# Remainders of split weights: subtracted on GpSimd in place of VectorE

## The chip, the cores and the metric

The kernel runs on one core of a Trainium2 chip. A core has a tensor engine (PE, with its weight loads shown apart as PEld), a vector engine (DVE, VectorE), a scalar engine (ACT, ScalarE), a GpSimd engine (POOL) and a sync engine (SP) that here issues the transfers. Each engine works through its own list of instructions in order; waits between engines are semaphores. The metric is the device time of one launch in microseconds (us), median of several runs. Three runs of the kernel before took 1236.23 us at the median (1233.64 to 1236.44).

## The reference

Four residual blocks on an input of 512 tokens by 1024 features, all in float32: attention (8 forgetting heads and 8 stick-breaking heads of width 64), a gated MLP of inner width 2816 with a causal depthwise convolution of three taps, a gated short convolution, and a second such MLP.

```python
h = x
for layer in range(2):
    h = h + (attention_mixer if layer == 0 else short_conv_mixer)(h, ...)
    h = h + conv_ffn(h, ffn_norm[layer], ffn_w_up[layer], ffn_conv[layer], ffn_w_down[layer])
# conv_ffn: u = causal_dwconv(rms_norm(h) @ w_up);  g, val = halves of u;  (silu(g) * val) @ w_down
# attention_mixer: one input projection, q and k normed per head, softmax with decay (FoX) or
#   stick-breaking weights, o @ w_out.  short_conv_mixer: (B * conv3(C * u)) @ w_out
```

Every product is `activation @ weight`, with weights that come from device memory once.

## The kernel before, in words

Activations stay on chip with features on partitions and the 512 tokens along the free axis. A float32 product runs on the tensor engine as three single-pass products of halves. A number x is split into hi, its rounding to a shorter float (float32r), and lo = x - hi, the remainder. Then x @ w is hi_x hi_w + lo_x hi_w + hi_x lo_w, summed in PSUM. `mm3` (lines 237 to 239) and `mm3_rhs` (lines 480 to 482) issue these three; the one that reads the weights' remainder is line 239 or line 481.

The weights come in 198 chunks of 128 partitions by 1024 numbers (16 have 896, two have 1056). `load` (lines 211 to 227) handles one chunk in three steps: SP issues the transfer into a buffer `raw` (line 220), ScalarE rounds it into `whi` (line 223), and VectorE subtracts to give `wlo` (line 226). Each of the three names has three buffers, so the rounding of a chunk waits until the tensor engine has read the last of the chunk three before. `weights` (line 229) hands out the next chunk and first calls `load` for those up to two chunks ahead (`AHEAD = 2`). A chunk is used for 24 products of 512 columns in most stages.

The stages in order of time: input and first projections (to about 50 us), attention (to about 305 us), the first MLP (to 674), the short convolution (to 854), and the second MLP (to the end, its down projection from 1101). That last down projection works on tokens by partition in two halves of 11 double rows each; the last three chunks of a half are used together, once for each of four blocks of tokens, so that chunk 10 of a half is needed two chunks' first uses after chunk 8 and not two whole chunks later.

In attention, generators of projections ("fillers") are woven between the score blocks by counted microseconds (`after`, `fill`, `spend`); which instruction stands where on an engine is set by the order in which the program emits them, and by the tile framework's own ordering. The weights of a block of 128 queries go from VectorE (line 596 for a forgetting head, lines 603 and 604 for a stick-breaking one) to the tensor engine, which transposes them (line 623); ScalarE and VectorE split the result into `pt` (lines 626 and 627), and line 642 and 643 multiply it with the values. Norms take an inverse root on VectorE (`rsqrt`, lines 300 to 318, some ten tiny instructions); the tensor engine spreads the first of them at line 278.

GpSimd has little to do: constants at the start, eight small transfers that it issues itself (lines 107 to 114), one clearing for the gates (line 434) and 64 clearings of a part of `pt` (line 617), each of which waits until the tensor engine has finished with that buffer.

Of the kernel before, what the change touches and what calls it, by code (L numbers as in the profile page):

```python
"""Two-layer hybrid decoder trunk on one core.

Activations stay on chip, features on partitions and tokens along the free axis.
Float32 products run on the tensor engine as three single-pass products of exact
halves: x = hi + lo with hi the rounding to float32r and lo the exact remainder,
x @ w = hi_x hi_w + lo_x hi_w + hi_x lo_w, summed in float32 in PSUM.
The RMS scale of a block's input is applied to the products, so that the tensor
engine doesn't wait for it.
"""
# [40 lines left out]
def trunk(  # L50
# [21 lines left out]
    def f32(ap):  # L72
        return ap.bitcast(F32)
# [25 lines left out]
    # a row a column of `gains`: the norms after the first and the conv taps  # L99
# [67 lines left out]
    def behind(later, earlier):  # L167
        """Issues `later` after `earlier`, of the same engine."""
        tc.add_manual_dep(
            later.ins, earlier.ins.name,  # L170
            mybir.DependencyInfo(mybir.DependencyClass.NoSync, mybir.DependencyReason.DATA), reason="order",
        )

    # ---- order of the tensor engine's work: `spend` counts the microseconds that were
    # emitted, `after` puts work that waits for other engines behind some of them, and
    # `fill` emits independent products in between ----
# [33 lines left out]
    def load(i, last=None):  # L210
        dram, k0, nk, parts = wanted[i]
        n = sum(parts[1::2])
        raw = wp.tile([P, CHUNK], F32, tag="raw", name=f"raw{i}")
        hi = wp.tile([P, CHUNK], F32R, tag="whi", name=f"whi{i}", bufs=3)
        lo = wp.tile([P, CHUNK], F32R, tag="wlo", name=f"wlo{i}", bufs=3)
        v = raw[:, 0:nk * n].rearrange("p (k c) -> p k c", c=n)
        to = 0
        for c0, width in zip(parts[::2], parts[1::2]):
            with nc.allow_non_contiguous_dma(reason="eight columns"):
                nc.sync.dma_start(  # L220
                    v[:, :, to:to + width], dram[k0 * P:(k0 + nk) * P, c0:c0 + width].rearrange("(k p) c -> p k c", p=P))
            to += width
        made = act.activation(hi[:, 0:nk * n], raw[:, 0:nk * n], AF.Copy)  # L223
        if last is not None:
            behind(made, last)
        dve.tensor_tensor(lo[:, 0:nk * n], raw[:, 0:nk * n], f32(hi[:, 0:nk * n]), op=ALU.subtract)  # L226
        return [t[:, 0:nk * n].rearrange("p (k c) -> p k c", c=n) for t in (hi, lo)]
# [7 lines left out]
    def mm3(acc, w, rhs, first, last):  # L235
        """acc += w.T @ rhs of two pairs of halves."""
# [10 lines left out]
    class Norm:  # L247
        """Gathers the squares of a block's input and gives its RMS scale by token:
        `col` [token, block] on partitions and `row` along the free axis on all of them."""
# [33 lines left out]
        def scaled(self, fn):  # L283
            """Runs what needs `row` when it is there."""
# [14 lines left out]
    def rsqrt(dst, v, n, name):  # L299
        """dst = v ** -0.5 by Newton's method."""  # L300
# [22 lines left out]
    def causal_conv(dst, src, tap):  # L323
        """dst[t] = tap(2) src[t] + tap(1) src[t-1] + tap(0) src[t-2]."""
# [68 lines left out]
    # ================= attention =================  # L393
# [4 lines left out]
    def choose():  # L398
        """Columns of 0 and 1 that pick the rows of `dl` and `dr`."""
# [25 lines left out]
    def log_gate():  # L425
        """The gates' log-sigmoid, its running sums on the partitions of `dl`."""
# [70 lines left out]
    def queries_keys(p):  # L497
        """Halves of the normed, gained keys and queries of heads 2p and 2p+1. A
        stick-breaking query keeps its scale apart, by token."""
# [63 lines left out]
    def logits(p, b):  # L563
        """Scores and decay of heads 2p and 2p+1 for 128 queries, and what follows up to the weights."""
# [44 lines left out]
    def turn(p, b, ws):  # L609
        """The weights, keys on partitions, in halves."""  # L610
# [19 lines left out]
    def weigh(p, half):  # L630
        """Weights by both halves of the values at once: a head's product has the one
        half on 64 partitions and the other on the rest, which are then added."""
# [98 lines left out]
    # decay: F_q - F_k of a forgetting head as a product of four rows by four. Head  # L731
    # 2p + e has them at 64 e + 4 j + p: (F_hi 1), (F_lo 1), (1 -F_hi), (1 -F_lo).
# [40 lines left out]
    # ================= gated MLP =================  # L773
# [38 lines left out]
    # ================= gated short convolution =================  # L812
# [32 lines left out]
    # ================= gated MLP, tokens on partitions at its end =================  # L845
# [59 lines left out]
```

## Time and profile before

| what | value |
|---|---|
| median of the runs (lowest to highest) | 1236.23 us (1233.64 to 1236.44) |
| profiled execution, its own time from first to last instruction (the span) | 1231.8 us |
| median of the runs above that span | 4.4 us |
| PE busy | 1214.5 us |
| DVE busy | 762.9 us |
| ACT busy | 500.7 us |
| POOL busy | 21.5 us |
| mean granted clock of the tensor engine | 0.997 |

Engines are named PE, PEld, DVE, ACT, POOL and SP. L226 is line 226 of the kernel. A group's row gives out<-in, shapes, count, busy us and mean ns of one instruction, then the idle time just before them and what ended it. A timeline's row gives start (us from the span's start), duration (us), engine, line, operation, out<-in and, in brackets, the idle time before it with what ended it. A row of the chain of work that ended last gives start, us, and what. Products are pipelined, so the busy time of one (0.39 us for 512 columns) is longer than the distance between two (0.23 us). The buffer names in rows of the profile leave out numbers.

### The profile page before, as it was taken

The page shows a single profiled execution, that of the slowest core. Times are in us where ns is not written, and L with a number is a line of the kernel's source. Part 1 is how long each engine was busy: PE and PEld are TensorE (multiplying, and loading weights), DVE is VectorE, ACT ScalarE, POOL GpSimd, SP SyncE. Part 2 cuts the span into 40 slices and gives each one's busy share as a digit, 9 for nine tenths or more (in the row PEclk, how much of TensorE's full clock was granted, in tenths as well). Part 3 has the DMA queues.
Part 4 walks back from the last instruction along what each step waited for, and adds up shares of the span by engine and source line. Part 5 has one row for each costly group of instructions (what it writes and reads, how often), then busy time and mean ns, then how long its engine had stood idle before and what let it go on. Part 6 is the DMA issues. An engine that isn't in the chain of part 4 may idle for free.

```text
span 1231.8 us, 14998 instructions
## 1 busy us (share of the span) xinstructions
PE 1214.5 (99%) x5861; PEld 987.9 (80%) x5861; DVE 762.9 (62%) x1256; ACT 500.7 (41%) x779; POOL 21.5 (2%) x104
## 2 busy tenths in 40 slices
PE   8999999999999999999999999999999999999998
PEld 7887878767888888888888888888888888888886
DVE  5786878887776777673333555555767776762222
ACT  6455665655443434342222222233444434342120
POOL 3000000000000000000000000000000000000000
PEclk9999999999999999999999999999999999999999
DMA  6312121212333332323333333332333333322330
GB/s 177 104 36 69 36 69 36 69 52 69 95 93 100 89 102 86 103 79 95 94 94 101 91 97 99 89 101 87 91 98 92 96 95 93 98 91 86 118 105 35
DMA packets 183463, 108.13 MB, mean 88 GB/s; under 512 B 4604, under 2 KB 176684, under 8 KB 183392
## 3 DMA queue, kind: packets, MB, share of 16 engines
q1 hardware_dynamic: 183136, 107.01, 29.5%
q8 instruction: 46, 0.75, 0.3%
q0 software_dynamic: 256, 0.16, 0.1%
q14 instruction: 25, 0.20, 0.0%
HBM read 105.06 MB, written 2.10 MB: 87 GB/s over the span
## 4 chain that ended last, share of the span: by engine, by line
PE 94%; DVE 4%; ACT 1%; DMA 1%; issue 0%; SPq 0%; DVEq 0%; ACTq 0%
PE psa L237 13%; PE psa L239 13%; PE psa L238 13%; PE psb L237 11%; PE psb L239 11%; PE psb L238 11%; PE psa L480 3%; PE psa L482 3%; PE psa L481 3%; PE psb L481 2%; PE psb L480 2%; PE psb L482 2%; PE psb L576 1%; DVE rest L603 1%; PE psc L623 1%; PE psa L642 1%
## 5 line engine op out<-in xcount | busy, mean ns | idle before, releaser
L223 ACT ACTIVATE whi<-raw 128x1024 fp32r<-128x1024 f32 (+1 forms) x198 | 208.3, 1053 | 365.9 <-PE psb L238 127.0
L226 DVE TENSOR_TENSOR wlo<-raw,whi 128x1024 fp32r<-128x1024 f32 (+1 forms) x198 | 240.1, 1213 | 162.3 <-ACT whi L223 161.4
L237 PE MATMUL psa<-hs_hi,whi 128*128 128x512 f32 x544 | 220.4, 405 | 0.5 <-DVE o L653 0.5
L239 PE MATMUL psa<-hs_hi,wlo 128*128 128x512 f32 x544 | 215.5, 396 | 0.0
L238 PE MATMUL psa<-hs_lo,whi 128*128 128x512 f32 x544 | 215.0, 395 | 0.0
L237 PE MATMUL psb<-hs_hi,whi 128*128 128x512 f32 x480 | 189.9, 396 | 0.0
L239 PE MATMUL psb<-hs_hi,wlo 128*128 128x512 f32 x480 | 189.8, 395 | 0.0
L238 PE MATMUL psb<-hs_lo,whi 128*128 128x512 f32 x480 | 188.8, 393 | 0.0
L328 DVE SCALAR_TENSOR_TENSOR u<-y,taps,u 128x510 f32<-128x510 f32 (+1 forms) x176 | 131.0, 747 | 3.0
L239 PEld LDWEIGHTS psa<-hs_hi,wlo 128*128 128x128 f32 x544 | 102.2, 188 | 24.0
L237 PEld LDWEIGHTS psa<-hs_hi,whi 128*128 128x128 f32 x544 | 102.7, 189 | 21.8 <-PE psb L582 0.6
L238 PEld LDWEIGHTS psa<-hs_lo,whi 128*128 128x128 f32 x544 | 102.6, 189 | 21.4
L238 PEld LDWEIGHTS psb<-hs_lo,whi 128*128 128x128 f32 x480 | 90.1, 188 | 21.4
L239 PEld LDWEIGHTS psb<-hs_hi,wlo 128*128 128x128 f32 x480 | 90.1, 188 | 21.4
L237 PEld LDWEIGHTS psb<-hs_hi,whi 128*128 128x128 f32 x480 | 90.3, 188 | 20.3
L779 DVE TENSOR_TENSOR y<-psb,nrow_n 128x512 f32<-128x512 f32 x44 | 30.4, 691 | 83.9 <-PE psb L239 83.9
L320 ACT ACTIVATE a<-u 128x512 fp32r<-128x512 f32 x44 | 27.8, 633 | 118.7 <-DVE u L784 118.7
L783 ACT ACTIVATE u<-u 128x512 f32<-128x512 f32 x44 | 27.8, 632 | 91.4 <-DVE u L328 91.4
L325 ACT ACTIVATE u<-y,taps 128x512 f32<-128x512 f32 x88 | 62.9, 717 | 0.0
L321 DVE TENSOR_TENSOR a<-u,a 128x512 fp32r<-128x512 f32 x44 | 30.4, 692 | 29.4 <-ACT a L320 29.4
L480 PE MATMUL psa<-whi,hs_hi 128*128 128x256 f32 (+1 forms) x128 | 38.6, 303 | 0.0
L482 PE MATMUL psa<-whi,hs_lo 128*128 128x256 f32 (+1 forms) x128 | 36.2, 283 | 0.0
(226 smaller groups left out, 1851.0 us busy)
## 6 DMA issues: line engine op xcount, KB each, us to landing
raw<-in_ffn_w_up SPq DMA_DIRECT2D x88, 512.0 KB, 3.8
raw<-in_ffn_w_down SPq DMA_DIRECT2D x30, 512.0 KB, 3.7
raw<-in_attn_w_in SPq DMA_DIRECT2D x24, 512.0 KB, 3.9
raw<-in_conv_w_in SPq DMA_DIRECT2D x24, 512.0 KB, 3.8
raw<-in_ffn_w_down SPq DMA_DIRECT2D x16, 448.0 KB, 3.7
raw<-in_attn_w_out SPq DMA_DIRECT2D x8, 512.0 KB, 3.4
raw<-in_conv_w_out SPq DMA_DIRECT2D x8, 512.0 KB, 3.9
x_tok<-in_x SPq DMA_DIRECT2D x4, 512.0 KB, 7.9
```

Source lines behind the costliest of these rows:

```text
L223: made = act.activation(hi[:, 0:nk * n], raw[:, 0:nk * n], AF.Copy)
L226: dve.tensor_tensor(lo[:, 0:nk * n], raw[:, 0:nk * n], f32(hi[:, 0:nk * n]), op=ALU.subtract)
L237: pe.matmul(acc, w[0], rhs[0], start=first, stop=False)
L238: pe.matmul(acc, w[0], rhs[1], start=False, stop=False)
L239: pe.matmul(acc, w[1], rhs[0], start=False, stop=last)
L321: dve.tensor_tensor(lo, src, f32(hi), op=ALU.subtract)
L325: act.activation(dst, src, AF.Copy, scale=tap(2))
L328: dve.scalar_tensor_tensor(dst[:, d:], src[:, 0:S - d], tap(j), dst[:, d:], op0=ALU.mult, op1=ALU.add)
L480: pe.matmul(acc, lhs[0], w[0], start=first, stop=False)
L481: pe.matmul(acc, lhs[0], w[1], start=False, stop=False)
L482: pe.matmul(acc, lhs[1], w[0], start=False, stop=last)
L779: dve.tensor_tensor(y, acc, norm.row, op=ALU.mult)
```

## The change

One line: the engine that subtracts `raw - whi` into `wlo`. The data, the sizes, the buffers and what is computed are the same; all 198 subtractions move. (The rest of the difference between the files takes comments away and is left out.)

```diff
         made = act.activation(hi[:, 0:nk * n], raw[:, 0:nk * n], AF.Copy)
         if last is not None:
             behind(made, last)
-        dve.tensor_tensor(lo[:, 0:nk * n], raw[:, 0:nk * n], f32(hi[:, 0:nk * n]), op=ALU.subtract)
+        pool.tensor_tensor(lo[:, 0:nk * n], raw[:, 0:nk * n], f32(hi[:, 0:nk * n]), op=ALU.subtract)
         return [t[:, 0:nk * n].rearrange("p (k c) -> p k c", c=n) for t in (hi, lo)]
```

GpSimd at the start of the program: the first six subtractions, among the constants, the small transfers into `spare` (lines 108 to 114) and the gates' clearing. The numbers behind names are buffers: `wlo_175` is the first chunk's remainder, `wlo_370` the fourth's.

```order
 L417 TENSOR_SCALAR cols<-cols 128x1
+L226 TENSOR_TENSOR wlo_175<-raw_173,whi_174 128x1024
+L226 TENSOR_TENSOR wlo_234<-raw_232,whi_233 128x1024
 L108 DMA spare<-in_ffn_norm 16x128
+L226 TENSOR_TENSOR wlo_240<-raw_238,whi_239 128x1056
 L109 DMA spare<-in_conv_norm 8x128
 L110 DMA spare<-in_conv_kernel 24x128
 L114 DMA spare<-in_ffn_conv 66x128 x4
+L226 TENSOR_TENSOR wlo_370<-raw_368,whi_369 128x1056
+L226 TENSOR_TENSOR wlo_426<-raw_424,whi_425 128x1024
+L226 TENSOR_TENSOR wlo_627<-raw_625,whi_626 128x1024
 L434 MEMSET fwide 128x512
```

The first two subtractions now stand ahead of all but one of the small transfers, and the third ahead of six of them.

GpSimd in attention, at the second pair of clearings (the one that is over at 91 us of the profile of before); `wlo_1349` and `wlo_1355` are the twelfth and thirteenth chunks' remainders.

```order
 L617 MEMSET pt_1275 128x128
 L617 MEMSET pt_1276 128x128
+L226 TENSOR_TENSOR wlo_1349<-raw_1347,whi_1348 128x1024
+L226 TENSOR_TENSOR wlo_1355<-raw_1353,whi_1354 128x1024
 L617 MEMSET pt_1434 128x128
 L617 MEMSET pt_1435 128x128
```

Two subtractions now stand between clearings that followed each other before; a clearing that waits for the tensor engine holds the subtractions written behind it.

VectorE in attention, at 71 us of the profile of before, where the eleventh chunk's remainder (`wlo_1000`) was made between the normed keys (`qn`) and their remainders (`qk_lo`):

```order
 L544 TENSOR_TENSOR qn_937<-qk_682,psc_932 128x512
-L226 TENSOR_TENSOR wlo_1000<-raw_998,whi_999 128x1024
+L544 TENSOR_TENSOR qn_948<-qk_723,psc_943 128x512
 L321 TENSOR_TENSOR qk_lo_940<-qn_937,qk_hi_939 128x512
-L544 TENSOR_TENSOR qn_948<-qk_723,psc_943 128x512
 L591 TENSOR_REDUCE top_979<-psb_966 128x1
+L321 TENSOR_TENSOR qk_lo_951<-qn_948,qk_hi_950 128x512
 L591 TENSOR_REDUCE top_987<-psb_967 128x1
```

The subtraction is gone from VectorE's list, and the second `qn` has moved up into its place. The other 197 go in the same way; at 184 us, for instance, one (the 22nd chunk's) stood in the middle of an inverse root's tiny instructions (between lines 316 and 312).

## The prediction, made before the changed kernel was run

> **What bounds the kernel now.** I read the page's busy times first, then busy time by stage, then the groups of the two weight steps, and last the few rows around the places where the tensor engine waits.
>
> ```profile
> span 1231.8 us, 14998 instructions
> core 0: us, PE busy (x) PEld busy (x) DVE busy (x) ACT busy (x) POOL busy (x), PEclk, DMA share, GB/s
> 0.00:50.00 50.00, 45.09 (x285) 39.68 (x286) 30.99 (x81) 29.90 (x47) 9.88 (x44) 0.97 0.55 152
> 50.00:266.00 216.00, 210.68 (x1404) 173.55 (x1403) 173.64 (x453) 128.34 (x292) 10.88 (x56) 1.00 0.19 55
> 266.00:310.00 44.00, 41.07 (x194) 32.83 (x194) 35.16 (x52) 24.46 (x42) 0.71 (x4) 0.96 0.22 64
> 310.00:1100.00 790.00, 790.00 (x3418) 638.99 (x3418) 489.77 (x639) 291.63 (x369) 0.00 (x0) 1.00 0.32 94
> 1100.00:1232.00 132.00, 127.67 (x565) 102.83 (x563) 33.35 (x33) 26.36 (x30) 0.00 (x0) 1.00 0.26 86
> L223 ACT ACTIVATE whi<-raw 128x1024 fp32r<-128x1024 f32 (+1 forms) x198 | 208.3, 1053 | 365.9 <-PE psb L238 127.0
> L226 DVE TENSOR_TENSOR wlo<-raw,whi 128x1024 fp32r<-128x1024 f32 (+1 forms) x198 | 240.1, 1213 | 162.3 <-ACT whi L223 161.4
> ```
>
> The tensor engine is the bound. From 310 to 1100 us, two thirds of the time, it is busy in every microsecond while DVE has 300 us to spare, so nothing that frees DVE can show there. What a faster DVE could give back lies in attention: 216.00 - 210.68 = 5.32 us of idle PE, and 44.00 - 41.07 = 2.93 us more up to 310, together 8.25, plus some 1.8 us for the granted clock of 0.96 in those 44. The change takes 240.1 us of work off DVE, 31% of what DVE does, and at best 10 us of it (8.25 + 1.8) were ever in the tensor engine's way. The row of L226 says the rest: DVE mostly stood waiting for the rounding (161.4 us). So the question is less what DVE gains than whether GpSimd is in time, and what it does to DVE while it works.
>
> **How long one subtraction takes on GpSimd.** No row of before shows one of this size there. The nearest:
>
> ```profile
> L617 POOL MEMSET pt<- 128x128 f32 x64 | 12.4, 222 | 221.3 <-PE psa L642 193.9 <-DVE inv L595 13.4 <-DVE ry_qk L316 13.0
> L434 POOL MEMSET fwide<- 128x512 f32 x1 | 0.5, 529 | 18.5 <-PE psc L542 18.5
> L409 POOL TENSOR_TENSOR both<-one 128x8 f32<-128x8 f32 x1 | 0.2, 213 | 0.0
> ```
>
> Writing alone costs (529 - 222) / 384 = 0.80 ns a column, and a two-operand instruction has 0.2 us of start-up. For 1024 columns that is 0.82 us a pass. If reads and write overlap fully, 1.02 us; if the two reads take turns, 1.84; if the write takes its turn too, 2.66. I take 2.25, midway between the last two, and keep 1.02 and 2.66 as ends. As a check from outside: the Trainium skill, "GPSIMD Engine Reference", section 3, gives 4497 ns for an addition of 2048 columns, so an estimate of some 2.25 us for half; no run here shows it yet.
>
> 198 x 2.25 = 446 us of a queue that was busy for 21.5, so its throughput is no limit. In the long stages nothing is due soon either: a chunk is rounded when the one three before is done, and two chunks of 24 products lie between. At 790 us / 3418 = 0.23 us a product that is 11 us, less 1.05 for the rounding. There the move costs nothing, hidden by the tensor engine's two chunks in hand. If VectorE were held for all of each subtraction there (142 chunks of 5.57 us in 790), it would lose 142 x (2.25 - 1.22) = 146 of its 300 us to spare: still cover.
>
> **Term 1, the last down projection.** Here the cover is gone. The rows are the rounding, the subtraction and the first product that reads it, at the first and the last of three such places (the second is at 1161.54):
>
> ```profile
> 1147.54 1.06 ACT L223 ACTIVATE whi<-raw 128x1024 fp32r<-128x1024 f32 x1 [4.54 <-PE psb L482]
> 1148.64 1.23 DVE L226 TENSOR_TENSOR wlo<-raw,whi 128x1024 fp32r<-128x1024 f32 x1 [4.37 <-ACT whi L223]
> 1150.38 0.40 PE L481 MATMUL psa<-wlo,a 128*128 128x512 f32 x1
> 1210.91 1.06 ACT L223 ACTIVATE whi<-raw 128x1024 fp32r<-128x1024 f32 x1 [4.54 <-PE psb L482]
> 1212.00 1.23 DVE L226 TENSOR_TENSOR wlo<-raw,whi 128x1024 fp32r<-128x1024 f32 x1 [4.37 <-ACT whi L223]
> 1213.74 0.40 PE L481 MATMUL psa<-wlo,a 128*128 128x512 f32 x1
> ```
>
> From the earliest start of the subtraction to the product are 1.74 us in both. At 2.25 the tensor engine waits 0.51 each time, 3 x 0.51 = +1.5 us. Ends: 0 at 1.02 us, 3 x 0.92 = +2.8 at 2.66. A quicker subtraction gains nothing here, since the product already ran on time.
>
> **Does GpSimd hold VectorE?** The rows that come nearest are clearings beside L596, VectorE's scaling of a forgetting head's weights:
>
> ```profile
> 102.22 1.20 POOL L617 MEMSET pt<- 128x128 f32 x4 [11.50 <-PE psa L642]
> 158.47 0.83 POOL L617 MEMSET pt<- 128x128 f32 x4 [11.83 <-PE psa L642]
> 102.08 0.49 DVE L596 TENSOR_SCALAR w<-w,inv 128x512 f32<-128x512 f32 x1
> 102.75 0.53 DVE L596 TENSOR_SCALAR w<-w,inv 128x512 f32<-128x512 f32 x1
> ```
>
> Four clearings take 0.83 us at 158 but 1.20 at 102, where they meet two L596 of 0.5 us: the two engines do take turns for something. Whether a subtraction that reads two tiles makes a VectorE instruction wait for all of it, no row shows. Bounds: VectorE loses nothing and is rid of 1.22 us, or it waits the whole 2.25, which is 1.03 more than it spent itself. I take the second for instructions that read two tiles on chip, because the row at 102 is a wait of nearly a whole instruction and not a slowing down, and keep both ends.
>
> The Trainium skill, "SBUF — State Buffer", section "Who interferes with whom", says that GpSimd and VectorE share a pair of ports as an exclusive lock, and that a VectorE instruction with two inputs in SBUF contends with a GpSimd one that reads SBUF; it also names the copy and scalar forms that the rows at 102 fit. By that rule the term below is +2.8 us; without any such turn-taking it would be -1.6.
>
> **Term 2, attention.** The places where the tensor engine now waits for VectorE with a subtraction just ahead in the chain of work:
>
> ```profile
> 71.27 1.22 DVE wlo L226
> 72.50 0.60 DVE qk_lo L321
> 77.61 0.61 PE L511 MATMUL psc<-head_ones,sq 128*128 128x2 f32 x4 [0.52 <-DVE pt L627]
> 183.95 1.23 DVE wlo L226
> 185.18 0.10 DVE ra_qk L312
> 191.49 0.49 PE L511 MATMUL psc<-head_ones,sq 128*128 128x2 f32 x3 [1.09 <-DVE pt L627]
> 276.31 1.06 ACT L223 ACTIVATE whi<-raw 128x1024 fp32r<-128x1024 f32 x1
> 277.90 0.41 DVE L321 TENSOR_TENSOR o_lo<-o,o_hi 128x256 fp32r<-128x256 f32 x1
> 278.84 0.68 DVE L627 TENSOR_TENSOR pt<-psc,pt 128x512 fp32r<-128x512 f32 x1
> 280.52 0.35 PE L643 MATMUL psa<-pt,v 128*128 128x256 f32 x1
> ```
>
> At the first two, VectorE's next instruction (L321 and L312) reads two tiles and follows the subtraction at once; held for 2.25 instead of spending 1.22, it hands on 1.03 us later each, and the tensor engine, which was already waiting, waits that much longer: +2.1. The third is new. Before, that chunk was subtracted late, after the block's last splits; on GpSimd it starts at 277.4, when the rounding ends, and L321 at 277.90 waits until 279.65, 1.75 us. The split behind it then ends at 279.52 + 1.75 = 281.27 instead of well ahead of L643 at 280.52: +0.75. Together +2.8. If nothing is held, the waits of 0.52 and 1.09 vanish, since 1.22 us leave their chain: -1.6. At the other places of idle PE in attention no subtraction stands right ahead, or the wait is small; I count nothing there.
>
> **Term 3, the start.** The fourth chunk's rounding meets the first inverse root:
>
> ```profile
> 24.04 1.10 ACT L223 ACTIVATE whi<-raw 128x1056 fp32r<-128x1056 f32 x1
> 25.40 0.16 DVE L316 SCALAR_TENSOR_TENSOR ncol_n<-rb_n,ry_n 128x4 f32<-128x4 f32 x1
> 26.70 0.60 PE L278 MATMUL psc<-ident,ncol_n 128*128 128x128 f32 x4
> ```
>
> The subtraction can start at 25.14 and hold L316 until 27.4; the tensor engine, due at L278 at 26.70, would get its input at about 27.6: +0.9. Without holding, 0. The last of GpSimd's small transfers fall behind three subtractions, at most 3 x 2.25 = 6.8 us:
>
> ```profile
> 19.70 2.09 POOL L114 DMA_DIRECT2D spare<-in_ffn_conv  x4
> 41.34 0.26 PE L142 MATMUL psc<-ident,spare 48*128 48x48 f32 x1
> ```
>
> Issued by 21.8 before, they are read at 41.34; those 20 us hide it, and it costs nothing.
>
> **The sum.** 1.5 + 2.8 + 0.9 = +5.2 us on the profiled span of 1231.8, so 1237.0. The median of the runs lies 4.4 us above that span; I carry this unchanged: 1236.2 + 5.2 = 1241.4.
>
> **Rivals.** *Nothing is held.* Then 1.5 - 1.6 + 0 = -0.1 us, 1236.1. For it speaks that clearings and plain two-tile instructions overlap freely in the timeline; against it the rows at 102.
>
> *VectorE's relief carries attention* (faster). 27 or so subtractions leave a stage where DVE is 80% busy (173.64 of 216). If all idle PE there and the half clock go, -10.0 + 1.5 = -8.5, 1227.7. It decides from 5.2 us of those 10 upward, for that pays term 1 and 0.3% of the time (3.7 us, about what a measurement here tells from no change). Against it: only 1.6 of the 8.25 stand at the two places above, where a subtraction leaves the chain.
>
> *GpSimd is much slower than 2.66 us,* through the short float it writes or by waiting itself for VectorE. Each microsecond above 2.25 costs one at three places each of terms 1 and 2 and one at the start, 7 in all: at 4 us, +17.5, 1253.7. Nothing in the rows asks for it.
>
> *The subtractions wait in GpSimd's queue.* The longest wait there is long:
>
> ```profile
> 73.78 0.35 POOL L617 MEMSET pt<- 128x128 f32 x2 [32.96 <-PE psa L642]
> 90.25 0.46 POOL L617 MEMSET pt<- 128x128 f32 x2 [0.48 <-PE psa L642]
> 92.73 1.06 ACT L223 ACTIVATE whi<-raw 128x1024 fp32r<-128x1024 f32 x1 [0.20 <-PE psa L482]
> ```
>
> A subtraction held for 33 us would stop the tensor engine for over 10. But the order puts `wlo_1000` ahead of the clearing at 73.78, and `wlo_1349`, behind the one that ends at 90.71, has its input only at 93.79. I give this price no chance of its own. The order also shows all 198 moved, so the change does what it says.
>
> **Chances.** VectorE held, 1238 to 1246: 0.58, of which 0.13 ends within 0.3%. Nothing held: 0.20, nearly all within 0.3% (0.17). Relief: 0.08, faster. A slow GpSimd: 0.14, slower. So faster 0.11, same 0.30, slower 0.59. The range 1233 to 1250 takes in the held case with both ends of the duration, the case of nothing held, and the nearer half of the slow one. The held case alone: 1238 to 1246.
>
> **What would show it.** L226 on POOL at 1.8 to 2.7 us; idle PE before L481 at three places near the end, half a microsecond each, put down to POOL; 310 to 1100 us unchanged at full PE; tiny VectorE instructions that last or wait 2 us beside a subtraction; idle PE from 50 to 310 at 10 to 12 us instead of 8.25. I am wrong if VectorE's two-tile instructions keep their durations beside POOL's L226, if attention gets shorter by more than 2 us, or if idle PE appears between 310 and 1100.

## The result, and the profile after

| kernel | median of the runs (lowest to highest) | profiled span |
|---|---|---|
| before | 1236.34 us (1233.64 to 1237.81) | 1231.8 us |
| after | 1275.37 us (1274.04 to 1277.40) | 1273.9 us |

The changed kernel takes 1.0322 times as long (95% interval 1.0305 to 1.0339), 39.0 us more. The forecast was 1241.4, with a range of 1233 to 1250. The direction was right, the size was not. The two profiled spans differ by 42.1 us, 3 more than the medians: by its span, the profile of before is of the quickest execution (1233.64 us), so differences between the two profiles overstate the change by about 3 us.

First the tensor engine's idle time over the same work. The windows of before and of after are cut some 8 us ahead of the first MLP's first gate, so that the same products, within three records, lie ahead of both cuts. Columns: the window and its length, busy us of PE, PEld, DVE, ACT and POOL with their instructions, then the granted clock, the DMA share and GB/s. The first fence is before, the second after.

```profile
0.00:310.00 310.00, 296.84 (x1881) 246.07 (x1882) 239.79 (x584) 182.69 (x380) 21.47 (x104) 0.99 0.25 72
310.00:1232.00 922.00, 917.67 (x3981) 741.81 (x3980) 523.12 (x672) 317.98 (x399) 0.00 (x0) 1.00 0.31 93
```

```profile
0.00:334.40 334.40, 301.79 (x1878) 248.15 (x1878) 238.96 (x549) 182.55 (x380) 106.71 (x139) 0.97 0.23 66
334.40:1274.00 939.60, 926.07 (x3983) 740.99 (x3983) 502.68 (x510) 311.61 (x399) 392.35 (x163) 1.00 0.31 92
```

The start and attention are 24.4 us longer. Idle time of the tensor engine makes 19.5 of it (334.40 - 301.79 = 32.61 after, 310.00 - 296.84 = 13.16 before), and 4.95 are products that ran slower (301.79 against 296.84 for the same work, clock 0.97 against 0.99). (Some 2.4 us of the 24.4 may be the difference between the two executions; see the table below.) The rest of the program is 17.6 us longer. VectorE did not become busier in either part: 238.96 against 239.79, and 502.68 against 523.12.

Now the groups of after, by line. Columns: busy us, mean ns of one, then the idle time before.

```profile
L226 POOL TENSOR_TENSOR wlo<-raw,whi 128x1024 fp32r<-128x1024 f32 (+1 forms) x198 | 477.0, 2410 | 694.9 <-ACT whi L223 673.1 <-PE psa L482 7.7 <-DVE ry_qk L316 7.3
L328 DVE SCALAR_TENSOR_TENSOR u<-y,taps,u 128x510 f32<-128x510 f32 (+1 forms) x176 | 250.2, 1424 | 109.2 <-ACT u L325 106.3
L259 DVE SCALAR_TENSOR_TENSOR hs_lo<-h,gains,hs_hi 128x512 fp32r<-128x512 f32 x24 | 46.8, 1949 | 19.6 <-ACT hs_hi L258 19.6
L596 DVE TENSOR_SCALAR w<-w,inv 128x128 f32<-128x128 f32 (+3 forms) x32 | 17.5, 547 | 0.8
L779 DVE TENSOR_TENSOR y<-psa,nrow_n 128x512 f32<-128x512 f32 x44 | 30.1, 684 | 2.8 <-ACT nrow_n L279 2.8
L627 DVE TENSOR_TENSOR pt<-psc,pt 128x128 fp32r<-128x128 f32 (+3 forms) x64 | 29.8, 484 | 11.4 <-ACT pt L626 11.1
L316 DVE SCALAR_TENSOR_TENSOR ncol_n<-rb_n,ry_n 128x4 f32<-128x4 f32 x4 | 3.1, 772 | 0.1
```

The same groups of before, where they differ or a comparison rests on them:

```profile
L328 DVE SCALAR_TENSOR_TENSOR u<-y,taps,u 128x510 f32<-128x510 f32 (+1 forms) x176 | 131.0, 747 | 3.0
L316 DVE SCALAR_TENSOR_TENSOR ncol_n<-rb_n,ry_n 128x4 f32<-128x4 f32 x4 | 0.6, 162 | 0.1
L259 DVE SCALAR_TENSOR_TENSOR hs_lo<-h,gains,hs_hi 128x512 fp32r<-128x512 f32 x24 | 17.9, 746 | 2.4 <-ACT hs_hi L258 2.4
L596 DVE TENSOR_SCALAR w<-w,inv 128x128 f32<-128x128 f32 (+3 forms) x32 | 12.1, 386 | 0.5
L627 DVE TENSOR_TENSOR pt<-psc,pt 128x128 fp32r<-128x128 f32 (+3 forms) x64 | 30.2, 485 | 7.8 <-ACT pt L626 7.3
```

A subtraction takes 2.41 us on GpSimd. VectorE's instructions with two inputs in tiles on chip last longer where they meet one, by up to that much: L328, the convolution's taps, takes 1424 ns on average (747 before), L259 takes 1949 (746), and of four tiny L316 on four columns one took 2.61 us, so that their mean is 772 ns (162 before). L596, which has one tile and one number for each partition, is longer too (547 ns, 386 before). L779 and L627, whose first input (`psa`, `psc`) lies in PSUM, kept their durations (L779 had 690 before), although six of the L627 began while a subtraction ran. L784 and the L321 of the gated product have two inputs on chip and kept their 0.69 us; none of these began while a subtraction ran.

Two places show what such a hold costs. VectorE and GpSimd of after, an inverse root at 196 us:

```profile
196.31 2.26 DVE L314 TENSOR_TENSOR rb_qk<-ra_qk,rh_qk 128x16 f32<-128x16 f32 x1
198.60 0.17 DVE L316 SCALAR_TENSOR_TENSOR ry_qk<-rb_qk,ry_qk 128x16 f32<-128x16 f32 x1
196.10 2.44 POOL L226 TENSOR_TENSOR wlo<-raw,whi 128x1024 fp32r<-128x1024 f32 x1 [7.26 <-DVE ry_qk L316]
205.28 0.83 PE L511 MATMUL psc<-head_ones,sq 128*128 128x2 f32 x6 [3.26 <-DVE pt L627]
```

An instruction on 16 columns, of the kind that takes 0.17 us in the next row, ends at 198.57 because the subtraction that started 0.21 us ahead of it ends at 198.54. Everything behind it on VectorE is 2.1 us late, and at 202 the tensor engine waits 3.26 us for VectorE's splits. At the place in before that the prediction named, 191.49, the same wait was 1.09.

The scaling of a forgetting head's weights, at 134 us of after:

```profile
134.15 2.03 DVE L596 TENSOR_SCALAR w<-w,inv 128x384 f32<-128x384 f32 x1
133.44 2.52 POOL L226 TENSOR_TENSOR wlo<-raw,whi 128x1024 fp32r<-128x1024 f32 x1 [6.92 <-ACT whi L223]
136.57 0.66 PE L542 MATMUL psc<-ident,qwide 128*128 128x128 f32 x4 [1.81 <-DVE pt L627]
```

The third row is a wait of 1.81 us at a place where before has none and the prediction counted nothing.

And the clock. Windows of after, around a wait of 1.81 us that ends at 84.56 and the one of 3.26 us above (the granted clock is the third number from the right):

```profile
84.60:86.60 2.00, 2.00 (x18) 1.86 (x20) 1.10 (x3) 0.13 (x1) 0.00 (x0) 0.99 0.03 8
86.60:90.00 3.40, 3.40 (x21) 3.17 (x18) 2.34 (x16) 0.92 (x4) 0.00 (x0) 0.50 0.00 0
206.00:209.40 3.40, 3.40 (x13) 2.82 (x13) 0.30 (x3) 0.00 (x0) 0.00 (x0) 0.51 0.00 0
1141.30:1144.70 3.40, 3.40 (x10) 2.63 (x9) 2.61 (x3) 1.26 (x2) 0.70 (x1) 0.50 0.40 125
```

Behind these waits the tensor engine runs at half its clock for 3.4 us at a time. Before has two of these stretches (at 11.0 and 277.2), after has five, the one at 298.2 twice as long: 20.5 us at half clock against 6.8. The difference is 13.7 us at half speed, or 6.8 us more of lost work.

The prediction said that nothing happens in the long stages. Here is the first MLP, by engines, of after:

```profile
485.27 2.40 POOL L226 TENSOR_TENSOR wlo<-raw,whi 128x1024 fp32r<-128x1024 f32 x1 [3.08 <-ACT whi L223]
491.42 2.41 POOL L226 TENSOR_TENSOR wlo<-raw,whi 128x1024 fp32r<-128x1024 f32 x1 [3.75 <-ACT whi L223]
496.92 2.41 POOL L226 TENSOR_TENSOR wlo<-raw,whi 128x1024 fp32r<-128x1024 f32 x1 [3.09 <-ACT whi L223]
489.76 0.64 ACT L320 ACTIVATE a<-u 128x512 fp32r<-128x512 f32 x1 [3.96 <-DVE u L784]
490.29 1.04 ACT L223 ACTIVATE whi<-raw 128x1024 fp32r<-128x1024 f32 x1
495.26 0.63 ACT L783 ACTIVATE u<-u 128x512 f32<-128x512 f32 x1 [2.78 <-DVE u L328]
495.80 1.04 ACT L223 ACTIVATE whi<-raw 128x1024 fp32r<-128x1024 f32 x1
485.83 3.16 DVE L328 SCALAR_TENSOR_TENSOR u<-y,taps,u 128x511 f32<-128x511 f32 x2 [1.72 <-ACT u L325]
489.03 0.69 DVE L784 TENSOR_TENSOR u<-u,u 128x512 f32<-128x512 f32 x1
492.51 2.65 DVE L328 SCALAR_TENSOR_TENSOR u<-y,taps,u 128x511 f32<-128x511 f32 x2 [0.80 <-ACT u L325]
```

and the same rows of ScalarE in before:

```profile
473.25 1.07 ACT L223 ACTIVATE whi<-raw 128x1024 fp32r<-128x1024 f32 x1 [1.07 <-PE psb L238]
478.85 1.06 ACT L223 ACTIVATE whi<-raw 128x1024 fp32r<-128x1024 f32 x1 [0.43 <-PE psa L238]
```

Before, the rounding (L223) waits for the tensor engine to let a buffer go: the tensor engine sets the pace. After, it no longer does; it waits behind L320 and L783 in ScalarE's own list, and these wait for VectorE. Following the rows gives a closed loop. The subtraction at 485.27 holds L328, which ends at 488.99; L784 ends at 489.72; L320 waits for it; the rounding behind L320 ends at 491.33; the next subtraction starts at 491.42 and holds the next L328 until 495.16; L783 waits for that; the rounding behind it ends at 496.84; the subtraction at 496.92 closes the circle. No step of it waits for the tensor engine. Two chunks take 496.92 - 485.27 = 11.65 us this way. The tensor engine needs 48 x 0.2315 = 11.1 us for them (780 us for 3370 products in a full stage). So the cover shrinks by half a microsecond with every pair. An estimate of it from these rows, 11.1 us for two chunks less 1.04 for the rounding and 2.41 for the subtraction, is 7.6 us, which lasts for 14 pairs at 0.54 us. From about the 14th of the layer's 22 pairs on (505 us) the tensor engine does wait for the remainder itself, every 11.6 us:

```profile
PEld psb L239 <- POOL wlo L226: 11.1, 16, 1.4
```

(us in total, times, longest, over both MLPs.)

At the end, the first of the three late products that term 1 was about, and (fourth row) the place where the last down projection's second accumulator starts while the gates lag behind:

```profile
1188.13 2.39 POOL L226 TENSOR_TENSOR wlo<-raw,whi 128x1024 fp32r<-128x1024 f32 x1 [3.19 <-ACT whi L223]
1189.55 0.40 PE L480 MATMUL psa<-whi,a 128*128 128x512 f32 x1
1190.57 0.50 PE L481 MATMUL psa<-wlo,a 128*128 128x512 f32 x1 [0.63 <-POOL wlo L226]
1139.98 0.50 PE L480 MATMUL psa<-whi,a 128*128 128x512 f32 x1 [2.61 <-DVE y L779]
```

Two products are 0.23 to 0.24 us apart when nothing is missing, so the product at 1190.57 is 1190.57 - 1189.55 - 0.24 = 0.78 us late (the idle time of 0.63 is smaller, since a product's record of 0.40 us is longer than that distance).

How late the changed kernel is against before at five marks, taken from start times of the same instructions in the two traces, with the experiments below in the same table. One profile each; up to the first MLP alone, profiles of kernels that are equal up to there differ by some 2.4 us (e6 against before), so the steps from column to column are read, and the first column only to that accuracy. The last column is from the medians.

| kernel | first MLP begins | short convolution begins | second MLP begins | last down projection's first sums | end | medians of the runs |
|---|---|---|---|---|---|---|
| after | 25.2 | 30.9 | 31.2 | 40.1 | 41.9 | +39.0 |
| e1_writes_only | 4.2 | 4.7 | 5.1 | 6.3 | 6.2 | +4.1 |
| e2_second_copy | 37.6 | 67.5 | 68.9 | 101.2 | 101.1 | +95.7 |
| e3_quarters | 14.4 | 14.6 | 14.8 | 15.6 | 16.3 | +13.7 |
| e9_one_input | 12.4 | 12.4 | 12.4 | 13.2 | 13.9 | +11.7 |
| e4_attention | 23.9 | 23.9 | 23.9 | 23.9 | 23.9 | +22.5 |
| e5_up | 2.6 | 6.5 | 6.8 | 12.0 | 12.0 | +13.1 |
| e6_rest | 2.4 | 2.7 | 2.7 | 3.7 | 5.4 | +3.9 |
| e7_up_first_half | 4.1 | 4.1 | 4.4 | 4.2 | 4.2 | +2.4 |
| e8_no_subtraction | -1.4 | -2.7 | -3.3 | -4.5 | -4.8 | -5.3 |

In the changed kernel the start and attention make 22 to 25 us (e4_attention: 22.5 by medians), the first MLP 5.7, the short convolution 0.3, the second MLP up to its last sums 8.9, and the last products 1.8.

### The profile page after: what moved, and what is told of

Same layout as the page of the kernel before. It is cut to its first block, busy times and chain, and to the rows that moved or that the text cites. A ratio compares the mean times of both kernels' runs of the same rounds, so it can differ in the third digit from the quotient of the medians.

```text
span 1273.9 us, 15079 instructions
## 1 busy us (share of the span) xinstructions
PE 1227.9 (96%) x5861; PEld 989.1 (78%) x5861; DVE 741.6 (58%) x1058; ACT 494.2 (39%) x779; POOL 499.1 (39%) x302
## 4 chain that ended last, share of the span: by engine, by line
PE 49%; issue 22%; POOL 15%; DVE 9%; ACT 3%; DMA 1%; POOLq 0%; SPq 0%; DVEq 0%; ACTq 0%
POOL wlo L226 15%; PE psa L237 7%; PE psa L238 7%; PE psa L239 7%; PE psb L237 7%; PE psb L239 7%; PE psb L238 7%; DVE rest L603 2%; PE psa L480 1%; PE psa L481 1%; PE psa L482 1%; PE psb L576 1%; DMA raw<-in_attn_w_in 1%; PE psc L623 1%; DVE hs_lo L259 1%
## 5 line engine op out<-in xcount | busy, mean ns | idle before, releaser
L226 POOL TENSOR_TENSOR wlo<-raw,whi 128x1024 fp32r<-128x1024 f32 (+1 forms) x198 | 477.0, 2410 | 694.9 <-ACT whi L223 673.1
L223 ACT ACTIVATE whi<-raw 128x1024 fp32r<-128x1024 f32 (+1 forms) x198 | 206.7, 1045 | 283.9 <-issue 82.8
L328 DVE SCALAR_TENSOR_TENSOR u<-y,taps,u 128x510 f32<-128x510 f32 (+1 forms) x176 | 250.2, 1424 | 109.2 <-ACT u L325 106.3
L320 ACT ACTIVATE a<-u 128x512 fp32r<-128x512 f32 x44 | 27.9, 633 | 166.8 <-DVE u L784 166.8
L783 ACT ACTIVATE u<-u 128x512 f32<-128x512 f32 x44 | 27.8, 633 | 120.3 <-DVE u L328 120.3
L325 ACT ACTIVATE u<-y,taps 128x512 f32<-128x512 f32 x88 | 62.8, 715 | 16.6 <-DVE y L779 16.6
L877 DVE TENSOR_TENSOR r<-psa,r 128x512 f32<-128x512 f32 x4 | 2.8, 692 | 100.0 <-PE psa L482 100.0
L259 DVE SCALAR_TENSOR_TENSOR hs_lo<-h,gains,hs_hi 128x512 fp32r<-128x512 f32 x24 | 46.8, 1949 | 19.6 <-ACT hs_hi L258 19.6
L321 DVE TENSOR_TENSOR a<-u,a 128x512 fp32r<-128x512 f32 x44 | 30.5, 693 | 29.5 <-ACT a L320 29.4
L480 PE MATMUL psa<-whi,hs_hi 128*128 128x256 f32 (+1 forms) x128 | 39.5, 308 | 1.8 <-DVE v L474 1.8
```

The lines of the kernel that those rows point to most:

```text
L226: pool.tensor_tensor(lo[:, 0:nk * n], raw[:, 0:nk * n], f32(hi[:, 0:nk * n]), op=ALU.subtract)
L259: dve.scalar_tensor_tensor(hs_lo[:, f, :], src, g, f32(hs_hi[:, f, :]), op0=ALU.mult, op1=ALU.subtract)
L320: act.activation(hi, src, AF.Copy)
L321: dve.tensor_tensor(lo, src, f32(hi), op=ALU.subtract)
L325: act.activation(dst, src, AF.Copy, scale=tap(2))
L328: dve.scalar_tensor_tensor(dst[:, d:], src[:, 0:S - d], tap(j), dst[:, d:], op0=ALU.mult, op1=ALU.add)
```

## Experiments

All were timed against the kernel before on the same chip (medians there 1234.7 to 1235.3). Two theories stood at first: *held* (while GpSimd reads a chunk, VectorE's instructions with two inputs on chip wait for the end of it) and *late* (VectorE is fine; the remainder just comes too late for the tensor engine, because 2.41 us and a wait in GpSimd's list come on top). Lines in a fence are those of the experiment's own file, a few lines further down than in before.

**1. GpSimd works as long, and only writes.** The remainders are zeros here: their part of every product is left out.

```diff
-        pool.tensor_tensor(lo[:, 0:nk * n], raw[:, 0:nk * n], f32(hi[:, 0:nk * n]), op=ALU.subtract)
+        m = nk * n
+        pool.tensor_copy(lo[:, 0:8], hi[:, 0:8])
+        pool.memset(f32(lo[:, 0:m]), 0.0)
+        pool.memset(f32(lo[:, 0:m]), 0.0)
+        pool.memset(f32(lo[:, 0:m // 2]), 0.0)
```

> GpSimd does not subtract: after the rounding it copies 8 columns and then clears the remainder's tile in three writes (about 0.95 + 0.95 + 0.53 us and a copy of 0.2, some 2.6 us together by the rate of the clearing of 512 columns, 0.53 us), so that it is as long and as late as the subtraction of 2.41 us but reads next to nothing. The remainders are zero in this run. Theory 'held' (a VectorE instruction that reads two tiles in SBUF waits for a running subtraction): L328's instructions are back at about 0.75 us from 1.42, and the time is at most 6 us above before (three late products near the end, 0.6 to 1.0 us each, and a few scalings of weights held by a write). Theory 'late' (the remainder is 1.2 us later and GpSimd's queue is longer, and that is what the tensor engine waits for): as slow as the change, 35 to 42 us above before.

Measured: 1239.40 us, ratio 1.0032 (1.0020 to 1.0044). The four GpSimd instructions take 0.22 + 0.95 + 0.95 + 0.52 = 2.64 us, longer than the subtraction, behind the same rounding and in the same places of GpSimd's list. From the groups:

```profile
L229 POOL MEMSET wlo<- 128x1024 f32 (+1 forms) x198 | 187.6, 947 | 11.1
L332 DVE SCALAR_TENSOR_TENSOR u<-y,taps,u 128x510 f32<-128x510 f32 (+1 forms) x176 | 131.5, 750 | 72.3 <-ACT u L329 69.4
L600 DVE TENSOR_SCALAR w<-w,inv 128x128 f32<-128x128 f32 (+3 forms) x32 | 15.4, 481 | 0.9
```

The taps (L328 of the other files, L332 here) are back at 750 ns, and 35 of the 39 us are gone. A remainder that is late by itself, queue included, is worth at most 4 us. *Late* falls; what costs is the reading. L596 (L600 here) is still held by writes, 481 against 386 ns. So are two more kinds with one tile as input: the copies of line 535 (517 ns on average, 424 before) and a tiny scalar step of the inverse root, line 306 (762 against 163).

**2. VectorE keeps the subtraction, GpSimd repeats three quarters of it** into a tile that nobody reads.

```diff
-        pool.tensor_tensor(lo[:, 0:nk * n], raw[:, 0:nk * n], f32(hi[:, 0:nk * n]), op=ALU.subtract)
+        dve.tensor_tensor(lo[:, 0:nk * n], raw[:, 0:nk * n], f32(hi[:, 0:nk * n]), op=ALU.subtract)
+        spare_lo = wp.tile([P, 768], BF16, tag="xlo", name=f"xlo{i}", bufs=1)
+        pool.tensor_tensor(spare_lo, raw[:, 0:768], f32(hi[:, 0:768]), op=ALU.subtract)
```

> VectorE subtracts as before the change, and GpSimd subtracts three quarters of the columns (768) once more into a tile that nobody reads, about 1.85 us each by 2.41 us for 1024. Theory 'held': slower than before by 20 to 45 us, although nothing waits for GpSimd's result, and L328 near 1.2 us. Theory 'late': within 2 us of before, L328 at 0.75.

Measured: 1331.04 us, ratio 1.0764 (1.0744 to 1.0783), +95.7: two to almost five times what was expected. The timeline says why:

```profile
543.09 1.84 POOL L228 TENSOR_TENSOR xlo<-raw,whi 128x768 bf16<-128x768 f32 x1 [3.81 <-ACT whi L223]
543.25 2.76 DVE L226 TENSOR_TENSOR wlo<-raw,whi 128x1024 fp32r<-128x1024 f32 x1
549.16 1.23 DVE L226 TENSOR_TENSOR wlo<-raw,whi 128x1024 fp32r<-128x1024 f32 x1 [1.11 <-ACT whi L223]
549.26 2.83 POOL L228 TENSOR_TENSOR xlo<-raw,whi 128x768 bf16<-128x768 f32 x1 [4.33 <-ACT whi L223]
```

One rounding releases both engines. Whoever is first runs at its own speed (1.84 on GpSimd, 1.23 on VectorE), and the other gets on when that ends: it lasts longer by 2.76 - 1.23 = 1.53 and 2.83 - 1.84 = 0.99 us, 0.15 us less than what was left of the first one. So the exclusion works both ways, and it is a wait, not a slowing down. Which of the two is first is sharp only to some 0.1 us in these records: in the changed kernel an L316 recorded at 26.08, 0.12 us ahead of a subtraction at 26.20, still lasted to that one's end. Work that nobody reads cost 7.6% of the time. The taps came to 1126 ns, near the 1.2 us expected; the expected time was too low because it took VectorE's subtraction as one more short instruction; it is the one the tensor engine waits for, and it now always meets GpSimd's.

**3. The subtraction in four pieces.**

```diff
-        pool.tensor_tensor(lo[:, 0:nk * n], raw[:, 0:nk * n], f32(hi[:, 0:nk * n]), op=ALU.subtract)
+        q = nk * n // 4
+        for j in range(4):
+            s = slice(j * q, (j + 1) * q)
+            pool.tensor_tensor(lo[:, s], raw[:, s], f32(hi[:, s]), op=ALU.subtract)
```

> The change with each subtraction cut into four of a quarter of the columns, about 0.7 us each (2.41 - 0.2 over 4, plus 0.2), 2.8 us a chunk. Theory 'held', instruction by instruction: a waiting VectorE instruction gets in after one piece, so L328's mean falls from 1.42 to 1.1 or less and the loss from 39 us to under 22. If the two engines instead share a rate, or if a waiting VectorE instruction is passed over by the next piece: L328 at 1.4 or more and 38 us or more of loss. Theory 'late': also 38 us or more, since each remainder is complete 0.4 us later.

Measured: 1249.08 us, ratio 1.0112 (1.0097 to 1.0127), +13.7.

```profile
L229 POOL TENSOR_TENSOR wlo<-raw,whi 128x256 fp32r<-128x256 f32 (+2 forms) x792 | 693.1, 906 | 469.0 <-ACT whi L223 455.1 <-PE psa L485 7.7 <-DVE ry_qk L319 6.2
L331 DVE SCALAR_TENSOR_TENSOR u<-y,taps,u 128x510 f32<-128x510 f32 (+1 forms) x176 | 180.7, 1030 | 73.3 <-ACT u L328 70.3
```

GpSimd is busy 1.45 times as long (693 against 477 us; a piece that has to wait for VectorE counts as busy), and the program gives back 25 of the 39 us: an instruction of VectorE that arrives now waits for the rest of one piece. The loop of the MLP is gone (14.4 to 14.6 over the first MLP, where the change itself goes from 25.2 to 30.9).

**4. One input in place of two.** GpSimd copies the rounded half twice in place of subtracting, so that the third part of every product is made from another number here.

```diff
-        pool.tensor_tensor(lo[:, 0:nk * n], raw[:, 0:nk * n], f32(hi[:, 0:nk * n]), op=ALU.subtract)
+        pool.tensor_copy(lo[:, 0:nk * n], hi[:, 0:nk * n])
+        pool.tensor_copy(lo[:, 0:nk * n], hi[:, 0:nk * n])
```

> GpSimd, in place of each subtraction, copies the rounded half of the chunk into the remainder's buffer twice, one whole copy after the other: the same waits and the same buffers, but each instruction has one input (the output is therefore not the reference's). From the clearings (0.95 us for 1024 columns) and the subtraction (2.41) I expect some 1.3 to 2.0 us for one copy. Theory A, VectorE's two-tile instructions are kept out by any GpSimd instruction that reads on-chip memory: the convolution's group on VectorE stays well above its 747 ns (I expect 950 to 1250, one copy long at most for one wait), and the time is 1250 to 1275. Theory B, only a GpSimd instruction with two inputs keeps them out: the group is back at about 750 ns as with clearings alone, and the time is 1235 to 1242.

Measured: 1246.74 us, ratio 1.0095 (1.0077 to 1.0113), +11.7, a little under the low end that theory A gave and well above the range of B. One copy took 1.06 us, less than the 1.3 to 2.0 expected.

```profile
L226 POOL CAST wlo<-whi 128x1024 fp32r<-128x1024 f32 (+1 forms) x198 | 209.2, 1057 | 678.4 <-ACT whi L223 674.7 <-PE psb L583 3.6
L227 POOL CAST wlo<-whi 128x1024 fp32r<-128x1024 f32 (+1 forms) x198 | 250.3, 1264 | 12.2
L329 DVE SCALAR_TENSOR_TENSOR u<-y,taps,u 128x510 f32<-128x510 f32 (+1 forms) x176 | 199.5, 1136 | 74.1 <-ACT u L326 71.2
```

One input is enough to hold the taps (1136 ns). The two copies together take nearly as long as the subtraction, 2.32 us (the second one's waits for VectorE counted in), and cost 11.7 us instead of 39. With experiment 3, where GpSimd's total grew and the loss fell, this says that the length of a single reading instruction sets the loss, not the engine's total: VectorE gets in between two of them.

The Trainium skill, "SBUF — State Buffer", section "Who interferes with whom", has this as its rule: a VectorE instruction with two inputs in SBUF contends with a GpSimd instruction that reads SBUF, not with one that only writes; one in a two-port mode contends with either; and whoever issues first keeps the shared pair for the whole instruction. Each part agrees with a row here: 1424 and 1136 ns beside reads and 750 beside writes, 481 for L596 beside writes, 2.76 against 2.83 us by the order of issue. That L596 runs in a two-port mode, no run here shows.

**5 to 7. The same change by stages.** Chunks 0 to 31 belong to attention, 32 to 75 and 132 to 175 to the up projections, the others to the rest.

```diff
-        pool.tensor_tensor(lo[:, 0:nk * n], raw[:, 0:nk * n], f32(hi[:, 0:nk * n]), op=ALU.subtract)
+        eng = pool if i < 32 else dve                                # e4_attention
+        eng = pool if 32 <= i < 76 or 132 <= i < 176 else dve        # e5_up
+        eng = pool if 76 <= i < 132 or i >= 176 else dve             # e6_rest
+        eng.tensor_tensor(lo[:, 0:nk * n], raw[:, 0:nk * n], f32(hi[:, 0:nk * n]), op=ALU.subtract)
```

> Only the first 32 chunks (first projections and attention) are subtracted on GpSimd, the other 166 on VectorE. Theory 'held': the first MLP starts 24 us late, as in the change, and nothing is lost afterwards: 22 to 27 us above before. Theory 'late': these remainders are done 7 us and more ahead of their use after the start, so at most 4 us above before.

> Only the 88 chunks of the two up projections of the MLPs are subtracted on GpSimd. The prediction had counted nothing there. Theory 'loop' (VectorE's held L328 delays ScalarE's next instruction, behind which the next rounding stands, so that a pair of chunks takes 11.65 us instead of 11.15; the lag grows by half a microsecond a pair until the cover of some 10 us is used up, and then the tensor engine waits): 11 to 15 us above before, all of it late in each up projection and at the start of what follows. If the loss were only in attention: within 2 us of before.

> Only the chunks of the short convolution and of the two down projections (78 of 198) are subtracted on GpSimd. Expected from the trace of the change: 0.6 to 0.9 us at each of three places near the end and 0.3 in the convolution, together 2 to 4 us above before. With e4 and e5 the sum should come near the 39 us of the whole change; a sum far from it would mean that the stages are not independent.

Measured: 1257.81 us (+22.5, ratio 1.0182, 1.0166 to 1.0197), 1247.82 (+13.1, ratio 1.0104, 1.0086 to 1.0121) and 1238.53 (+3.9, ratio 1.0030, 1.0018 to 1.0041). 22.5 + 13.1 + 3.9 = 39.5 against 39.0 for the whole: within their intervals (about 2 us each) the stages add up. In the table they do so less well: from the first MLP on, the changed kernel loses 16.7 us, e5_up and e6_rest 9.4 and 3.0. The profile of e5_up is 2.0 us under the median, and of these three profiles only the changed kernel's has the half clock at 1141 (1.7 us); that a stage feeds another by a microsecond is not excluded. In attention it is not VectorE's amount of work; the window 50 to 320 of e4_attention and of before:

```profile
50.00:320.00 270.00, 247.03 (x1552) 202.04 (x1553) 202.92 (x465) 146.44 (x326) 71.62 (x85) 0.97 0.18 51
```

```profile
50.00:320.00 270.00, 261.75 (x1645) 214.64 (x1644) 214.59 (x522) 156.62 (x338) 11.59 (x60) 0.99 0.20 57
```

VectorE is busy for 203 of 270 us with the holds counted in, in a window that, being late, holds less of the work (1552 products against 1645). The chain through it is longer at each hold; its throughput is not used up.

**8. Half of each up projection.** Is the loop right, or do the 44 chunks of a layer each cost the same share? Only the first 22 chunks of each layer go to GpSimd.

```diff
-        pool.tensor_tensor(lo[:, 0:nk * n], raw[:, 0:nk * n], f32(hi[:, 0:nk * n]), op=ALU.subtract)
+        eng = pool if 32 <= i < 54 or 132 <= i < 154 else dve
+        eng.tensor_tensor(lo[:, 0:nk * n], raw[:, 0:nk * n], f32(hi[:, 0:nk * n]), op=ALU.subtract)
```

> GpSimd subtracts only the first 22 chunks (11 of 22 pairs) of each up projection. Theory 'loop': the lag reaches 11 x 0.5 = 5.5 us, stays inside the cover and is worked off in the second half: at most 1 us above before, although half the subtractions are as in e5. If each subtraction cost its own share: half of e5, 5.5 to 7.5 us.

Measured: 1237.07 us, ratio 1.0018 (1.0009 to 1.0028), +2.4. In the table the delay stays between 4.1 and 4.4 from the first MLP's beginning to the end, where e5_up steps by 3.9 and 5.2 in the two MLPs. Half of the chunks cost almost nothing within the MLPs, as the loop says (the cover is only being used up), and equal shares would have cost half of 13.1. The 2.4 are still more than the 1 us that was expected at most. They lie before the first MLP gets going: between the first split of the norm ahead of it (L259) and its first gate this run falls back by 1.9 us, and there the first subtractions of its weights meet that norm.

**9. No subtraction at all.** All remainders of weights are one tile of zeros, made once; the third part of every product works on zeros. It bounds what VectorE's relief could ever have brought.

```diff
-        lo = wp.tile([P, CHUNK], F32R, tag="wlo", name=f"wlo{i}", bufs=3)
+        lo = no_lo
...
-        pool.tensor_tensor(lo[:, 0:nk * n], raw[:, 0:nk * n], f32(hi[:, 0:nk * n]), op=ALU.subtract)
```

> No subtraction at all, on either engine: the products read one tile of zeros as the remainder. This measures the most that VectorE's relief can be worth. The prediction's bounds were 1.6 us (two waits) and 10 us (all idle time in attention and the half clock). I expect 2 to 5 us below before; 8 or more would mean that the relief was worth having and was lost to the held instructions, 1 or less that there was nothing to win.

Measured: 1229.34 us, ratio 0.9953 (0.9938 to 0.9967), -5.3. That is a little more than the 2 to 5 expected. In the table 1.4 us are gained by the first MLP; the tensor engine's idle time up to there is 11.8 us against 13.2 in before, 1.3 less. Against the profile of e6_rest, which is equal to before up to there, it is 3.8. VectorE's relief in attention is thus worth 1.4 to 3.8 us, less than the 5.2 at which the rival would decide. The rest comes evenly over stages in which the tensor engine is never idle: in 130 us of the first MLP the products start 231.1 ns apart here, 232.2 in before, and 232.4 in experiment 1, whose remainders are zeros too. So the zeros are not the reason; what the reason is stays open.

## Why the prediction was wrong

**The mechanism was right, the places where it acts were not.** "Held" was the forecast case, for instructions that read two tiles on chip (one tile twice counts as well: the L312 that term 2 named, and the scan L603, 1085 ns on average against 816). Experiments 1 and 4 show it. The scaling L596 stood in its rows as a sign of taking turns, but no term had a price for it. The rival *nothing is held* falls with L328 at 1424 ns. *VectorE's relief carries attention* falls with experiment 9: 1.4 to 3.8 us, where it needed 5.2. *GpSimd is much slower* falls: 2.41 us against 2.25, which by the prediction's own 7 us for each microsecond is 1.1 us. The wait in GpSimd's queue did no harm that could be seen: the clearings of experiment 1 stand in the same list, last longer, and cost 4.1 us in all.

**Term 1** (+1.5) is a term that was a little too small: three products late by 0.78 are 2.3 us; the table shows 1.8 between its last two marks, for the second and third of them, and e6_rest +3.9 for this and everything else outside attention and up projections. Of the missing 0.27 at each place 0.14 is the longer subtraction.

**Term 3** (+0.9): L316 took 2.61 us at 26.08 (0.16 before) and the tensor engine waited 1.20 for it. Right. A second wait at the start, 1.51 us at 50.51 behind a split (L321) held for 2.2 us, had no term.

**Term 2** (+2.8) is the first step that failed, with its sentence "At the other places of idle PE in attention no subtraction stands right ahead, or the wait is small; I count nothing there". At its first two places the waits became 1.81 for 0.52 and 3.26 for 1.09, +1.3 and +2.2 where +1.03 each was said. At the third the hold came as told (2.17 us for a split that took 0.41), but it cost 1.57 us where 0.75 was said: the tensor engine waits, at 300.50, for the addition behind that split (L669), three products ahead of the one that the term named.

```profile
297.67 2.17 DVE L321 TENSOR_TENSOR o_lo<-o,o_hi 128x256 fp32r<-128x256 f32 x1
```

So the term is 5.0 us in place of 2.8. What it left out is larger. Other waits of the tensor engine in attention each stand behind a held instruction, at places where before has none or a small one: 1.75 us at 74.23 behind an L312, 1.81 and 1.11 at 136.57 and 150.90 behind L596, 1.19 (0.27 before) and 1.56 at 193.34 and 272.74 behind splits (L321), 1.78 at 220.31 behind a scan (L603). That is 8.9 us more; with the 5.0 and the two waits at the start, 16.6 of the 19.5 us of idle time have their place.

The places of the term were found in the trace of before, by asking where a subtraction stood ahead of a wait. That asks where VectorE was *rid* of something. Where it is *held* is decided by when GpSimd runs, which is whenever a rounding ends, and VectorE, at work for 174 of 216 us in attention before, is then mostly within some chain of softmax, inverse root or split: of the 35 subtractions that ran ahead of the first MLP in after, 23 held an instruction, by 0.5 to 2.4 us. The windows show +24.4 us up to the first MLP, 19.5 of idle time and 4.95 of slower products. e4_attention repeats it alone, with +22.5 by medians.

The half clock is part of the same failure. The prediction used the clock only for a gain (1.8 us in the window with 0.96). Three more stretches, and a double length of one, took 6.8 us away, about 5 of it ahead of the first MLP.

**"There the move costs nothing, hidden by the tensor engine's two chunks in hand"** is the second step that failed. Its arithmetic held: VectorE was busy for 471 of the 780 us from 320 on, holds included. It weighed throughput against throughput, and the cover against one subtraction. The cover is a stock, however, and what matters is whether something refills it. A rounding stands in ScalarE's list behind an instruction that waits for VectorE (L320 or L783), VectorE waits for GpSimd, and GpSimd for the rounding. This loop takes 11.65 us for a pair, the tensor engine 11.1, so the stock runs out after some 14 pairs. Measured: 13.1 us in e5_up, 5.7 and 8.9 in the two MLPs of the changed kernel; of the 8.9, 2.6 are the wait at 1139.98 and 1.7 the half clock behind it. Experiment 8, which stops at 11 pairs, and experiment 3, whose loop is shorter, both lose nothing there. The short convolution and the first down projection cost 0.3 us in e6_rest, as said.

**What stays open:** how much of the time lost in attention each kind of held instruction makes. By their groups, the scans lasted 8.9 us longer in all (34.7 against 25.8), the splits of `o` 8.9, the scaling 5.4, the splits of `qn` 3.5, and the inverse roots of queries and keys 4.1, but no run held one kind alone. Open too is why some waits are followed by half a clock and others not, and why the products of experiment 9 follow each other faster in stages that the tensor engine fills.

No version here beats the kernel before with the whole computation done: doing no subtraction at all gains 5.3 us, of which 1.4 to 3.8 are VectorE's relief in attention, and the mildest form in which GpSimd does any of the subtractions, e7_up_first_half, is 2.4 us slower.

## What to carry to other kernels

Before work goes to an idle GpSimd, list VectorE's instructions with two inputs on chip, and its scalings: in this kernel each can be made to wait for a whole GpSimd instruction that reads, wherever the two meet, so price the move by the length of one GpSimd instruction at every chain that VectorE is part of, not by its busy time; if it must be, cut it into pieces (39 us became 14). When a stage is covered by buffers, look for a ring of in-order engines that no longer includes the bound, and compare its period with the bound's: half a microsecond in 11 emptied two chunks of cover within one layer. In a latency-bound stage ask where the moved work will *run*, not where it used to stand.

## What was not expected of the hardware

- The exclusion between VectorE and GpSimd is complete and works both ways: an instruction of 16 columns lasted 2.26 us beside a subtraction, and GpSimd's own 1.84 us became 2.83 when VectorE was first. A second copy that nobody read cost 95.7 us.
- A GpSimd instruction with one input holds VectorE as well (taps at 1136 ns beside copies of 1.06 to 1.26 us); clearings don't (750 ns), except for kinds with one tile as input: the scaling L596 (481 against 386), copies (517 against 424) and scalar steps.
- A single wait of the tensor engine of 1.81 us, ended at 84.56, was followed 2 us later by 3.4 us at half clock. Not every such wait was: after the one that ended at 136.57 the clock stayed at 1.00 (100 to 150 us). The Trainium skill, "TensorE: Matmul & The Clock Gate", section "HAM oscillation — how this bites in real kernels", has the rule that gaps above some 3.4 us are to be avoided. Here single waits of half that length were followed by half a clock at some places; that they alone brought it about is not shown. The length of a stretch, 3.4 us, agrees with the window that the page's Part 1 gives.
